# Stick-breaking items from the last query block down, and zeros and sums of h moved behind the head

## The chip, the cores and the metric

The kernel runs on one core of one Trainium2 chip. The metric is the device time of one launch, in microseconds (us). TensorE is called PE below, VectorE DVE, ScalarE ACT, GpSimd POOL, and SyncE, which issues nearly all DMAs, SP.

## The reference

The program is a trunk of two layers over 1024 tokens with 1024 features, in float32. Each layer is

```
h      = rmsnorm(x);  proj = h @ w_in            # q, k, v of two mixers, and two gates
o_a    = dilated sliding-window attention, 12 heads in 3 groups (dilation 1, 4, 16)
o_b    = stick-breaking attention, 4 heads:
         z = q k^T / 8,  for keys s < t only
         A[t,s] = sigmoid(z_ts) * prod_{s<j<t} (1 - sigmoid(z_tj))
         o = A v
x      = x + (sigmoid(g_a)*(o_a @ w_br_a) + sigmoid(g_b)*(o_b @ w_br_b)) @ w_o
x      = x + (gelu(causal_conv(h2 @ w_up_a)) * (h2 @ w_up_v)) @ w_down,   h2 = rmsnorm(x)
```

The product over j runs from the key to the query: for a query block, what a key's weight needs lies at later keys, and the scan runs from the last key down.

## The kernel before

Matmuls are made exact enough by splitting each operand into a high and a low part (`hi`, `lo`): ACT casts the high part, DVE or POOL subtracts it from the source for the low part, and PE runs three matmuls per pair (`product`). PE's instructions run in the order in which the Python program issues them (a manual schedule); DVE's, ACT's, POOL's and SP's order is set by a list scheduler with priorities, and each engine then works in order.

A layer's mixer has these parts.

- **Start and head.** In layer 0, `first` loads x, turns and normalises it into `h` (tiles `hh`, `hl`, one pair per half n of the tokens); a small tile `g_raw` holds the norm's gains. `head` makes values `v_ps` and the keys and queries (`kq_ps`, `q_ps`) of the first two stick heads by `kq_half`, one half of the tokens at a time, and writes them to DRAM (`sk`, `sq`, `sv`). In layer 1 the head is woven into the last products of the FFN before it (`d_ps`) and the norm (`nrm_t`).
- **Sums of h.** `block_sums` makes combinations of blocks of `h` for a seven-product (Strassen-like) scheme. Each of the first two series has four sums of three POOL instructions (`h_sum`), then a cast on ACT (`t_hi`) and a subtraction on DVE (`t_lo`). They are entries of `dense.side`, and one is taken with each `aside()`; before the change the head's loop calls `aside()` as well.
- **Zeros.** `zeros` (layer 0) fills a tile `none` with zeros and writes it to the unused parts of `sq` (8 DMAs) and `tk` (8 DMAs) in DRAM. It is called before the first part. `none` and `g_raw` share one buffer (tag "ot").
- **Dense units.** `Dense` hands out pieces of the big projections (`g_ps` plain, then `i_a`, `i_b`, `i_c` in seven products). One piece of six matmuls is a share. `advance(rate)` is called after each small step of attention and lets `rate` shares run; so dense matmuls fill PE while the attention's chain of ACT and DVE goes on.
- **Items.** `attend` runs 16 stick items, named by head u and pair qp of query blocks, then 4 windowed items (`near_item`, dilation 1), then 16 of the dilated groups. An item has scores and micro steps: `turn` (PE transposes 128 x 128 blocks into `sb_t`, then a split into parts) and `apply` (PE multiplies with the values into `sb_o`). The next item is scored while the present one is turned. A stick item's score gives `z`; ACT makes `beta` = sigmoid(z) and `stay` = sigmoid(-z); DVE scans `stay` from the last key down in chunks of up to 512 keys and multiplies `beta` by it.
- **Fetches.** `dense.fetch` issues the DMAs of an item's keys, queries and values (tiles `kv`, `slots`) once their data and room are there, and marks them as there (`FB`, `FN`) after `LEAD` = 6 further shares. A new head's rows are fetched only when all four items of the head before it are scored.

Before the change a head's items go qp = 0, 1, 2, 3, so from the shortest (256 keys) to the longest (1024), and an item's turns go from the first keys up. The first turn thus needs all scans of its two rows. `pair_v` transposes values (`v_t`), which shares a bank with the scores.

Of the kernel before, what the change touches and what calls it, by code (L numbers as in the profile page):

```python
# [16 lines left out]
P = 128  # L17
# [20 lines left out]
ET = mybir.EngineType  # L38
NO_SYNC = mybir.DependencyInfo(mybir.DependencyClass.NoSync, mybir.DependencyReason.DATA)
# [3 lines left out]
RATE = (1.0, 1.2, 1.35, 1.4)  # L43
RATE_N = 0.85
RATE_T = 0.8
PLAIN = 4
LEAD = 6
AHEAD_B = 3
# [10 lines left out]
def trunk_kernel(ctx, tc, x, norm1, w_in, b_gate, w_br, w_o, norm2, w_up, conv_w, conv_b, w_down, norm_f, out, depth=None, probe=None):  # L59
# [156 lines left out]
    class Dense:  # L216
# [4 lines left out]
        def __init__(self):  # L221
            self.main, self.plain, self.seven, self.done = [], [], [], set()
            self.side, self.later, self.hooks = [], {}, []
            self.now = self.nxt = None
            self.due, self.count = 0.0, 0
            self.started = False
            self.scored = self.applied = self.kq = self.v = 0
            self.rows, self.near, self.free = 0, 0, [0] * 4
            self.b = self.n = 0
# [25 lines left out]
        def fetch(self):  # L255
# [313 lines left out]
    def in_parts(c, scale, hi, lo, x):  # L569
        if c:  # L570
            act.mul(hi, x, scale)
            dve.scalar_tensor_tensor(lo, x, scale, f32(hi), ALU.mult, ALU.subtract)
        else:
            act.copy(hi, x)
            dve.tensor_tensor(lo, x, f32(hi), ALU.subtract)

    def kq_half(c, w, n):
# [3 lines left out]
        in_parts(c, SCALE, hi, lo, o)  # L581
# [52 lines left out]
    def fetch_row(j):  # L634

        u, qp = divmod(j, 4)
        if j == 0:
            R["kv"] = sb.tile([P, 2, T], F32R, tag="xa", bufs=4, name="kv")
        if "slots" not in R:
# [3 lines left out]
        nc.sync.dma_start(f32(R["slots"][:, j % 4]), sq[u][:, :, t])  # L643
        nc.sync.dma_start(f32(R["kv"][:, 1, t]).rearrange("p (b c) -> p b c", c=P), sv[u][:, 2 * qp : 2 * qp + 2, :])

    def fetch_whole(v):
        kv = R["kvn", v] = sb.tile([P, 2, T], F32R, tag="xa", bufs=4, name="kv")
        nc.sync.dma_start(f32(kv[:, 0, :]), sk[4 + v])
        for k in range(2):
            nc.sync.dma_start(f32(R["slots"][:, :, k, :]), sq[4 + v][:, k, :].rearrange("p (m c) -> p m c", c=256))  # L650
        nc.sync.dma_start(f32(kv[:, 1, :]).rearrange("p (b c) -> p b c", c=P), sv[4 + v])

    def stick_item(dense, u, qp):
        q, k, v = R["slots"][:, qp], R["kv"][:, 0, :], R["kv"][:, 1, :]
        pr, s = divmod(u, 2)
        rows, st, shared = {}, {}, {}

        def score(a):
            i = 2 * qp + a
            L = P * (i + 1)  # L660
# [4 lines left out]
            for c0 in range(0, L, 512):  # L665
                w = min(512, L - c0)
                z = bank("s", "z")
                scores(z[:, :w], *(q[:, x, a * P : a * P + P] for x in range(2)), k[:, c0 : c0 + w])
                with tc.high_priority(offset=AHEAD):
                    if c0 + w == L:  # L670
                        dve.tensor_tensor(z[:, w - P : w], z[:, w - P : w], mask_b, ALU.add)
                    act.activation(bt[:, c0 : c0 + w], z[:, :w], AF.Sigmoid)
                    act.activation(sv[:, c0 : c0 + w], z[:, :w], AF.Sigmoid, scale=-1.0)
# [8 lines left out]
        def scans(most=9):  # L682

            while SCANS and most:
                most -= 1
                bt, sv, c0, c1, L, soon = SCANS.pop(0)
                rev = sv[:, c0:c1][:, ::-1]
                with tc.high_priority(offset=AHEAD) if soon else nullcontext():
                    one = dve.tensor_tensor_scan(rev, rev, zero[:, 0:1].to_broadcast([P, c1 - c0]), 1.0 if c1 == L else sv[:, c1 : c1 + 1], ALU.mult, ALU.add)
                    if "dve" in LAST:  # L690
                        tc.add_manual_dep(one.ins, LAST["dve"], NO_SYNC, reason="in turn")
                    k0, k1 = max(0, c0 - 1), c1 - 1
                    dve.tensor_tensor(bt[:, k0:k1], bt[:, k0:k1], sv[:, k0 + 1 : k1 + 1], ALU.mult)

        def blocks(kb):

            return [(j, a) for j in range(2) for a in range(2) if kb + j <= 2 * qp + a]

        def turn(kb):
            if kb == 0:  # L700
                scans()
            tp = bank("t", "sb_t")
            todo = blocks(kb)
# [3 lines left out]
            scans(max(1, len(SCANS) - 2))  # L707

        def apply(kb):
            last = kb == 2 * qp  # L710
            if kb == 0:
                shared["o"] = bank("o", "sb_o")[:, :256]
            o = shared["o"]
            for j in range(2):
                c = P if last and j else 0
                for p in (0, 1):
# [4 lines left out]
                        start=(kb == 0 and j == 0 and p == 0),  # L721
                        stop=(last and j == 1 and p == 1),
                        skip_group_check=True,
                    )
            if qp == 3:
                dense.free[kb // 2] = u + 1
            if last:
# [5 lines left out]
        return sc, [(lambda kb=kb: turn(kb), lambda kb=kb: apply(kb)) for kb in range(0, 2 * qp + 2, 2)]  # L733
# [240 lines left out]
    def block_sums():  # L974
# [4 lines left out]
        def first(t, a, b, i):  # L979
# [6 lines left out]
            if "last" in keep:  # L986
                tc.add_manual_dep(one.ins, keep["last"], NO_SYNC, reason="one sum after the other")
            pool.tensor_tensor(r, r, f32(ah), ALU.add)
# [28 lines left out]
        series(set(), 3, lambda i: first(3, b22, b12, i), 4, 3)  # L1017
        series(set(), 1, lambda i: first(1, b12, b11, i), 4, 3)
        for i in range(4):
            todo.append((set(), lambda i=i: less(b22, i)))  # L1020
        series(set(), 2, lambda i: i or new_s(2), 0, 1)
        series({"plain"}, 4, lambda i: further(4, b21, i), 1, 1)
        return todo

    def zeros():
# [3 lines left out]
        for u in range(8):  # L1029
# [1033 lines left out]
```

## Time and profile before

| | |
|---|---|
| median of 3 runs | 2790.09 us (2789.9 to 2792.63) |
| profiled execution, own time | 2786.15 us |
| its span, first to last instruction | 2784.3 us |
| PE busy | 2658.9 us, 95% |
| DVE busy | 2082.1 us, 75% |
| ACT busy | 1343.6 us, 48% |
| POOL busy | 675.7 us, 24% |
| mean granted clock of PE | 0.987 |

The profile's views used below are: the page (busy times), the waits (whom an engine waited for: total us, times, longest), the timeline (start, duration, engine, line, output and inputs; in brackets the idle time before and what ended it), the view by stages (busy time per engine in a stretch, with the granted PE clock), and groups of instructions (busy us, mean ns, then idle time before them). Line numbers in them are those of the kernel before.

### The profile page before, as it was taken

How to read it: one execution, taken by the hardware profiler on the slowest of the kernel's cores; microseconds unless marked ns; L12 is line 12 of the kernel's file. 1: busy time of each engine (PE TensorE's matmuls, PEld its weight loads, DVE VectorE, ACT ScalarE, POOL GpSimd, SP SyncE). 2: the span in 40 equal slices, each digit the busy share in tenths (PEclk: the TensorE clock that was granted, in tenths of full speed). 3: DMA queues.
4: the chain of work that ended last, by engine and by line, in shares of the span. 5: the costliest groups of instructions: out<-in, count | busy, mean ns of one | idle time of the engine just before them, and what ended most of it. 6: DMA issues, size and time to landing. Idle time of an engine off the chain costs nothing. (4 is left out here: it accounts for less than half of the span.)

```text
span 2784.3 us, 36703 instructions
## 1 busy us (share of the span) xinstructions
PE 2658.9 (95%) x12780; PEld 2211.2 (79%) x12780; DVE 2082.1 (75%) x3151; ACT 1343.6 (48%) x2488; POOL 675.7 (24%) x481
## 2 busy tenths in 40 slices
PE   5899999999999999999979999999899999999999
PEld 5777777877888888888868777878788888888888
DVE  4677776568589889897656777656767888988965
ACT  4355555556455555532333555645554555554225
POOL 4300101103214334331060011011122334443210
PEclk9999999999999999999989999999999999999999
DMA  8545576566334444498534566656643344446863
GB/s 230 167 112 155 145 198 200 187 199 210 95 110 142 142 162 163 150 349 307 189 103 130 136 170 164 192 175 201 232 145 87 121 159 165 138 153 239 320 263 121
DMA packets 423140, 489.22 MB, mean 176 GB/s; under 512 B 26036, under 2 KB 339756, under 8 KB 421164
## 3 DMA queue, kind: packets, MB, share of 16 engines
q1 hardware_dynamic: 422940, 486.88, 54.5%
q8 instruction: 101, 1.65, 0.3%
q14 instruction: 83, 0.68, 0.1%
q10 hardware_dynamic: 16, 0.00, 0.0%
HBM read 311.62 MB, written 175.18 MB: 175 GB/s over the span
## 5 line engine op out<-in xcount | busy, mean ns | idle before, releaser
L144 DVE TENSOR_TENSOR w_lo<-up_a,w_hi 128x512 fp32r<-128x512 f32 x240 | 236.7, 992 | 20.1 <-ACT w_hi L139 20.1
L1058 POOL TENSOR_TENSOR u<-in_a 128x512 f32<-128x512 f32 x32 | 45.2, 1411 | 818.3 <-DMA in_a<-in_w_in_dram 275.8
L139 ACT CAST w_hi<-up_a 128x512 fp32r<-128x512 f32 x240 | 149.4, 622 | 183.8 <-PE u_a L969 45.9
L1699 DVE TENSOR_TENSOR x<-x,d_ps 128x512 f32<-128x512 f32 (+1 forms) x228 | 151.8, 671 | 77.5 <-PE d_ps L1693 76.0
L1430 POOL TENSOR_TENSOR cv<-cv 128x512 f32<-128x512 f32 x88 | 131.8, 1508 | 249.4 <-DVE cv L1425 139.5
L139 ACT CAST w_hi<-in_a 128x512 fp32r<-128x512 f32 x192 | 119.1, 620 | 150.2 <-PE i_a L969 50.4
L144 DVE TENSOR_TENSOR w_lo<-in_a,w_hi 128x512 fp32r<-128x512 f32 x192 | 139.2, 725 | 45.6 <-ACT w_hi L139 45.3
L144 DVE TENSOR_TENSOR g<-cv,g 128x512 fp32r<-128x512 f32 x154 | 151.7, 986 | 5.2 <-ACT g L139 2.8
L1691 PE MATMUL d_ps<-gd_in,w_hi 128*128 128x512 f32 (+1 forms) x340 | 130.4, 384 | 1.3 <-ACT w_hi L139 0.6
L1693 PE MATMUL d_ps<-gd_in,w_lo 128*128 128x512 f32 (+1 forms) x340 | 129.8, 382 | 0.0
L1692 PE MATMUL d_ps<-gd_in,w_hi 128*128 128x512 f32 (+1 forms) x340 | 129.7, 382 | 0.0
L968 PE MATMUL u_a<-hh,w_hi 128*128 128x512 f32 x320 | 124.7, 390 | 0.3
L970 PE MATMUL u_a<-t_hi,w_lo 128*128 128x512 f32 x320 | 124.5, 389 | 0.0
L970 PE MATMUL u_a<-hh,w_lo 128*128 128x512 f32 x320 | 124.5, 389 | 0.0
L969 PE MATMUL u_a<-t_lo,w_hi 128*128 128x512 f32 x320 | 124.5, 389 | 0.0
L969 PE MATMUL u_a<-hl,w_hi 128*128 128x512 f32 x320 | 124.5, 389 | 0.0
L968 PE MATMUL u_a<-t_hi,w_hi 128*128 128x512 f32 x320 | 124.5, 389 | 0.0
L144 DVE TENSOR_TENSOR w_lo<-w_raw,w_hi 128x512 fp32r<-128x512 f32 x96 | 71.0, 742 | 62.1 <-ACT w_hi L139 61.6
L139 ACT CAST g<-cv 128x512 fp32r<-128x512 f32 x154 | 94.9, 616 | 39.6 <-POOL cv L1430 29.2
L1691 PE MATMUL d_ps<-gd_in,wd 128*128 128x512 f32 (+1 forms) x292 | 113.9, 390 | 0.0
L1693 PE MATMUL d_ps<-gd_in,wd 128*128 128x512 f32 (+1 forms) x292 | 112.8, 386 | 0.0
L1692 PE MATMUL d_ps<-gd_in,wd 128*128 128x512 f32 (+1 forms) x292 | 112.8, 386 | 0.0
(393 smaller groups left out, 8581.1 us busy)
## 6 DMA issues: line engine op xcount, KB each, us to landing
gd<-g SPq DMA_DIRECT2D x154, 512.0 KB, 3.5
gd_in<-gd SPq DMA_DIRECT2D x154, 512.0 KB, 6.5
up_a<-in_w_up_dram SPq DMA_DIRECT2D x80, 512.0 KB, 5.3
in_a<-in_w_in_dram SPq DMA_DIRECT2D x64, 512.0 KB, 4.9
t_kq<-tk SPq DMA_DIRECT2D x32, 768.0 KB, 4.6
wd_raw<-in_w_down_dram SPq DMA_DIRECT2D x22, 1024.0 KB, 12.0
gin<-gs SPq DMA_DIRECT2D x32, 512.0 KB, 4.5
w_raw<-in_w_o_dram SPq DMA_DIRECT2D x64, 256.0 KB, 2.9
```

Source lines behind the costliest of these rows:

```text
L139: one = act.copy(hi, src)
L144: two = dve.tensor_tensor(lo, src, f32(hi), ALU.subtract)
L968: pe.matmul(o, w[0][:, c], rh, start=(first and i == 0), stop=False, skip_group_check=True)
L969: pe.matmul(o, w[0][:, c], rl, start=False, stop=False, skip_group_check=True)
L970: pe.matmul(o, w[1][:, c], rh, start=False, stop=(last and i == 3), skip_group_check=True)
L1058: pool.tensor_tensor(u2, a11, a21, ALU.subtract)
L1430: return lambda: pool.tensor_tensor(dst, a, b, ALU.subtract)
L1691: pe.matmul(o[:, sub], wh[:, c], gh[:, sub], start=(i == 0 and k in (0, 4, 5)), stop=False, skip_group_check=True)
L1692: pe.matmul(o[:, sub], wh[:, c], gl[:, sub], start=False, stop=False, skip_group_check=True)
L1693: pe.matmul(o[:, sub], wl[:, c], gh[:, sub], start=False, stop=(i == m - 1), skip_group_check=True)
L1699: dve.tensor_tensor(x, x, o[:, sub], ALU.add)
```

## The change

Seven edits go together.

1. A head's items go qp = 3, 2, 1, 0, and an item's turns from the last keys down; score chunks are cut from the last key, the last chunk of each row is scanned first, and a turn makes only the scans that its own keys need.
2. A head's keys and queries are fetched by quarters, each as soon as the item that used that quarter last is scored; values by quarters, when the last product with them is issued. An item still waits for all four quarters of its head.
3. The zero part of the queries is set once by a memset in `slots`, and only the other half is fetched; the 8 zero writes to `sq` go.
4. The remaining 8 zero writes (`tk`) become a side entry behind the first three series of sums, instead of the first thing issued.
5. The sums' first POOL instruction waits for the head's last `in_parts` (a real wait), and the head's loops no longer call `aside()`. Within the two series the steps are closer together (lag 3, gap 2 instead of 4, 3).
6. Windowed items are marked as fetched after 9 shares instead of 6; `pair_v` turns after 3 shares instead of 2, and its two copies get high priority.
7. Rates: 1.0, 1.15, 1.25, 1.3 for stick items (1.0, 1.2, 1.35, 1.4 before), 0.75 instead of 0.8 for the dilated groups.

```diff
+LEAD_N = 9
...
             def row(j):
-                u, qp = divmod(j, 4)
-                return j < 16 and {f"K{u}", f"V{u}"} <= self.done and (u == 0 or (self.rows >= 4 * u and self.free[qp] >= u))
+                return j < 16 and f"K{j // 4}" in self.done and self.rows >= j - 3
+
+            def row_v(j):
+                return j < self.b and self.free[3 - j % 4] >= j // 4
...
+            while row_v(self.bv):
+                fetch_values(self.bv)
+                self.bv += 1
             while whole(self.n):
                 fetch_whole(self.n)
-                self.at(LEAD, lambda v=self.n: self.done.add(f"FN{v}"))
+                self.at(LEAD_N, lambda v=self.n: self.done.add(f"FN{v}"))
...
-        in_parts(c, SCALE, hi, lo, o)
+        LAST["head"] = in_parts(c, SCALE, hi, lo, o).ins.name
...
     def fetch_row(j):
-        u, qp = divmod(j, 4)
+        u, qp = j // 4, 3 - j % 4
...
+            pool.memset(f32(R["slots"][64:128, :, 1, :]), 0.0)
         t = slice(256 * qp, 256 * qp + 256)
         nc.sync.dma_start(f32(R["kv"][:, 0, t]), sk[u][:, t])
-        nc.sync.dma_start(f32(R["slots"][:, j % 4]), sq[u][:, :, t])
+        nc.sync.dma_start(f32(R["slots"][:, qp, 0, :]), sq[u][:, 0, t])
+        nc.sync.dma_start(f32(R["slots"][0:64, qp, 1, :]), sq[u][0:64, 1, t])
+
+    def fetch_values(j):
+        u, qp = j // 4, 3 - j % 4
+        t = slice(256 * qp, 256 * qp + 256)
         nc.sync.dma_start(f32(R["kv"][:, 1, t]).rearrange("p (b c) -> p b c", c=P), sv[u][:, 2 * qp : 2 * qp + 2, :])
...
     def stick_item(dense, u, qp):
...
-            for c0 in range(0, L, 512):
-                w = min(512, L - c0)
+            for c1 in range(L, 0, -512):
+                c0 = max(0, c1 - 512)
+                w = c1 - c0
...
-            for c1 in range(L, 0, -512):
-                SCANS.append((bt, sv, max(0, c1 - 512), c1, L, False))
-            if L <= 512:
-                scans()
+                (SCANS if c1 == L else left).append((shared, bt, sv, c0, c1, L))
             if a:
-                dense.rows = 4 * u + qp + 1
+                SCANS.extend(left)
+                dense.rows += 1
...
         def turn(kb):
-            if kb == 0:
-                scans()
+            while any(x[0] is shared and x[4] > kb * P for x in SCANS):
+                scans(1)
...
-            scans(max(1, len(SCANS) - 2))
+            scans(2)
...
         def apply(kb):
-            last = kb == 2 * qp
-            if kb == 0:
+            first = kb == 2 * qp
+            if first:
                 shared["o"] = bank("o", "sb_o")[:, :256]
+                dense.free[qp] = u + 1
...
-        return sc, [(lambda kb=kb: turn(kb), lambda kb=kb: apply(kb)) for kb in range(0, 2 * qp + 2, 2)]
+        return sc, [(lambda kb=kb: turn(kb), lambda kb=kb: apply(kb)) for kb in range(2 * qp, -2, -2)]
...
             if "last" in keep:
                 tc.add_manual_dep(one.ins, keep["last"], NO_SYNC, reason="one sum after the other")
+            else:
+                tc.add_manual_dep(one.ins, LAST["head"], SYNC, reason="after the first projections")
...
-        series(set(), 3, lambda i: first(3, b22, b12, i), 4, 3)
-        series(set(), 1, lambda i: first(1, b12, b11, i), 4, 3)
+        series(set(), 3, lambda i: first(3, b22, b12, i), 3, 2)
+        series(set(), 1, lambda i: first(1, b12, b11, i), 3, 2)
...
         series(set(), 2, lambda i: i or new_s(2), 0, 1)
+        todo += more
...
     def zeros():
...
-        for u in range(8):
-            nc.sync.dma_start(sq[u][64:128, 1, :], none[0:64].rearrange("p a b -> p (a b)"))
...
-            act.copy(vv[:, :, :, 0:64], tw)
-            dve.tensor_tensor(vv[:, :, :, 64:128], tw, f32(vv[:, :, :, 0:64]), ALU.subtract)
+            with tc.high_priority(offset=AHEAD):
+                act.copy(vv[:, :, :, 0:64], tw)
+                dve.tensor_tensor(vv[:, :, :, 64:128], tw, f32(vv[:, :, :, 0:64]), ALU.subtract)
...
-            dense.at(2, lambda: turn(c, n, f))
+            dense.at(3, lambda: turn(c, n, f))
...
-        dense.side = block_sums()
+        dense.side = block_sums([(set(), zeros)] * (l == 0))
...
             for _ in units:
-                dense.aside()
+                pass
         else:
-            zeros()
...
             for _ in first_units:
-                dense.aside()
+                pass
...
-            items.append((f"B{j // 4}{j % 4}", [f"FB{j}"], [], RATE[j % 4], lambda j=j: stick_item(dense, j // 4, j % 4)))
+            items.append((f"B{j}", [f"FB{j // 4 * 4 + 3}"], [], RATE[3 - j % 4], lambda j=j: stick_item(dense, j // 4, 3 - j % 4)))
```

More of the change, by code (lines that the diff above doesn't have):

```diff
@@ L571, in in_parts @@
             act.mul(hi, x, scale)
[L572 to L575, printed above, removed]
+            return dve.scalar_tensor_tensor(lo, x, scale, f32(hi), ALU.mult, ALU.subtract)
+        act.copy(hi, x)
+        return dve.tensor_tensor(lo, x, f32(hi), ALU.subtract)
     def kq_half(c, w, n):
@@ L679, in score, with scans @@
+                (SCANS if c1 == L else left).append((shared, bt, sv, c0, c1, L))
             if a:
-                dense.rows = 4 * u + qp + 1
-        def scans(most=9):
+                SCANS.extend(left)
+                dense.rows += 1
+        def scans(most):
             while SCANS and most:
                 most -= 1
-                bt, sv, c0, c1, L, soon = SCANS.pop(0)
+                _, bt, sv, c0, c1, L = SCANS.pop(0)
                 rev = sv[:, c0:c1][:, ::-1]
[L688 to L693, printed above, removed]
@@ L695, in blocks @@
-        def blocks(kb):
-            return [(j, a) for j in range(2) for a in range(2) if kb + j <= 2 * qp + a]
+                one = dve.tensor_tensor_scan(rev, rev, zero[:, 0:1].to_broadcast([P, c1 - c0]), 1.0 if c1 == L else sv[:, c1 : c1 + 1], ALU.mult, ALU.add)
+                if "dve" in LAST:
+                    tc.add_manual_dep(one.ins, LAST["dve"], NO_SYNC, reason="in turn")
+                k0, k1 = max(0, c0 - 1), c1 - 1
+                dve.tensor_tensor(bt[:, k0:k1], bt[:, k0:k1], sv[:, k0 + 1 : k1 + 1], ALU.mult)
@@ L720, in apply @@
                         shared[kb][p][:, 256 * j : 256 * j + 256 - c],
-                        start=(kb == 0 and j == 0 and p == 0),
-                        stop=(last and j == 1 and p == 1),
+                        start=(first and j == 0 and p == 0),
+                        stop=(kb == 0 and j == 1 and p == 1),
                         skip_group_check=True,
                     )
-            if qp == 3:
-                dense.free[kb // 2] = u + 1
-            if last:
+            if kb == 0:
                 out_ = small("ob")[0:64, 0:256]
```

30 lines of the change are left out of this document (15 added, 15 removed).

## The prediction

> **What bounds the kernel now.** I read the page's busy times first, then the waits of the tensor engine (PE), then the timeline where each long wait ends.
>
> ```profile
> span 2784.3 us, 36703 instructions
> PE 2658.9 (95%) x12780; PEld 2211.2 (79%) x12780; DVE 2082.1 (75%) x3151; ACT 1343.6 (48%) x2488; POOL 675.7 (24%) x481
> ```
>
> PE is busy 95% of the span, and the change issues the same matmuls (the built program's order lists as many rows on PE before and after, and the same dense matmuls per layer). So what can be won is PE's idle time, 2784.3 - 2658.9 = 125 us, and stretches in which PE runs at a lower clock. Who ends the idle time:
>
> ```profile
> PE warm L1967 <- DMA g_raw<-in_norm_dram: 25.7, 1, 25.7
> PE sb_t L705 <- DVE beta L693: 17.7, 14, 3.2
> PE nrm_t L506 <- DVE nrm L459: 11.9, 2, 11.8
> PE z L613 <- DMA kv<-sk: 9.5, 2, 5.2
> PE z L613 <- DVE vv L1153: 7.3, 6, 2.0
> PE kq_ps L176 <- DVE vb L550: 5.8, 1, 5.8
> PE kq_ps L177 <- POOL hl L523: 5.5, 2, 4.7
> PE v_t L1149 <- DVE u L1088: 5.2, 4, 2.4
> PE v_ps L176 <- DVE kq_l L572: 5.0, 1, 5.0
> ```
>
> These nine rows make 93.6 us, and the edits touch all of them. After a long wait PE also runs slowly. In the view by stages (columns: length, then busy time of PE, its weight loads, DVE, ACT, POOL, then granted clock, DMA share, GB/s):
>
> ```profile
> 74.00:100.00 26.00, 15.18 (x69) 13.58 (x68) 20.63 (x21) 5.49 (x10) 18.56 (x12) 0.74 0.41 111
> 450.00:466.00 16.00, 10.82 (x45) 8.66 (x44) 6.72 (x14) 4.29 (x11) 0.13 (x1) 0.79 0.61 175
> 1410.00:1462.00 52.00, 34.71 (x155) 29.42 (x154) 23.25 (x29) 15.79 (x27) 30.69 (x22) 0.77 0.40 114
> 1818.00:1834.00 16.00, 11.68 (x48) 9.42 (x47) 7.52 (x14) 4.63 (x11) 1.33 (x2) 0.79 0.70 206
> ```
>
> Length times the missing clock gives what the slow clock costs behind these waits: 26 x 0.26 = 6.8 us (head of layer 0), 52 x 0.23 = 12.0 us (entry of layer 1), and 16 x 0.21 = 3.4 us each in front of a windowed item.
>
> **Part 1, zeros out of the start.** The queues at the start:
>
> ```profile
> 0.74 0.39 SPq L1880 DMA_DIRECT2D xr<-in_x_dram  x1
> 1.95 8.87 SPq L1030 DMA_DIRECT2D sq<-none  x8
> 10.86 9.99 SPq L1034 DMA_DIRECT2D tk<-none  x8
> 20.90 2.40 SPq L1883 DMA_DIRECT2D w_raw<-in_w_in_dram  x2
> 24.58 0.58 ACTq L1869 DMA_DIRECT2D g_raw<-in_norm_dram  x1
> 29.69 0.27 PE L1967 MATMUL warm<-ident,g_raw 8*128 8x8 f32 x1 [25.74 <-DMA g_raw<-in_norm_dram]
> 34.80 0.39 PE L176 MATMUL v_ps<-w_hi,hh 128*128 128x256 f32 x1
> ```
>
> Sixteen writes of zeros hold SP from 1.95 to 20.85 us, ahead of the first weights. `g_raw` is on ACT's queue, but it lies in the same single buffer (tag "ot") as the tile of zeros, so its load starts at 24.58 and lands at 29.69, 5.1 us later. After the change the eight `sq` writes are gone and the eight `tk` writes stand behind the sums of h. `g_raw` can then start at about 0.7 and land by 5.8; the two weights start at about 1.2 instead of 20.90, 19.7 us earlier. From `g_raw` to the first projection lie 34.80 - 29.69 = 5.1 us, so the projection would start near 10.9 by `g_raw`, near 15.1 if the weights' place alone counted (34.80 - 19.7). The weights' casts were through well before 34.80, so I take `g_raw`: **-24 us** (19.7 to 26).
>
> **Part 2, sums of h behind the head.** In layer 0:
>
> ```profile
> 67.88 0.39 PE L178 MATMUL q_ps<-hh,kq_w 128*128 128x512 f32 x1
> 73.37 0.62 ACT L139 CAST t_hi<-h_sum 128x512 fp32r<-128x512 f32 x1 [3.38 <-POOL h_sum L989]
> 76.05 0.59 ACT L571 ACTIVATE kq_h<-q_ps 128x512 fp32r<-128x512 f32 x1
> 78.28 0.68 DVE L572 SCALAR_TENSOR_TENSOR kq_l<-q_ps,kq_h 128x512 fp32r<-128x512 f32 x1
> ```
>
> `q_ps` is complete at 68.3, but ACT reads it only at 76.05: ACT works in order and stood at `t_hi` casts that wait for POOL's sums. DVE's `kq_l` ends at 78.96, and PE's 5.0 us wait ends with it. The 5.8 us wait for `vb` has the same origin. With the sums held back by the dependency on the head's last `in_parts`, both go, and the slow clock behind them: 5.0 + 5.8 + 6.8 = 17.6; I leave 1 us: **-16.6** (10 to 17.6). Layer 1, where the sums mix with the norm:
>
> ```profile
> 1403.61 0.39 PE L1693 MATMUL d_ps<-gd_in,w_lo 128*128 128x512 f32 x1
> 1414.08 0.62 ACT L139 CAST t_hi<-h_sum 128x512 fp32r<-128x512 f32 x1 [4.74 <-POOL h_sum L989]
> 1414.52 0.67 DVE L1699 TENSOR_TENSOR x<-x,d_ps 128x512 f32<-128x512 f32 x1
> 1419.54 0.68 DVE L1699 TENSOR_TENSOR x<-x,d_ps 128x512 f32<-128x512 f32 x1
> ```
>
> PE's last `d_ps` ends at 1404.0, yet DVE adds it at 1419.54, queued behind work on sums that waits for ACT and POOL. That is the 11.8 us wait at `nrm_t`; the two waits for POOL's `hl` (5.5) come from `hl` queued between sums. 11.8 + 5.5 + 12.0 = 29.3; the chain of `hl` may become late next, so I leave 1.3: **-28** (20 to 29.3).
>
> Of the moved work every instruction still runs: per layer 24 sums on POOL, eight casts on ACT, eight subtractions on DVE, now beside the first stick items. What that costs there:
>
> ```profile
> L988 POOL TENSOR_TENSOR h_sum<-h_sum,hh 128x512 f32<-128x512 f32 x8 | 12.9, 1612 | 0.6
> L144 DVE TENSOR_TENSOR t_lo<-h_sum,t_hi 128x512 fp32r<-128x512 f32 x7 | 7.9, 1147 | 3.8 <-ACT t_hi L139 3.6
> 125.61 0.68 DVE L144 TENSOR_TENSOR t_lo<-h_sum,t_hi 128x512 fp32r<-128x512 f32 x1
> ```
>
> Beside POOL's sums DVE's `t_lo` takes 1.15 us, alone 0.68: 0.47 more. The built order puts about 30 DVE instructions of that kind (subtractions, scans, products of two SBUF tiles) beside the sums in layer 0: 30 x 0.47 = 14 us of DVE. Layer 1 starts its sums 11 us earlier relative to the items and overlaps less. Some of this lies in DVE's idle time, so I take **+8** for both layers (0 to 28). The Trainium skill ("GPSIMD Engine Reference", Specifications) says that GpSimd's SBUF interfaces are shared with VectorE, contended by instructions with two SBUF inputs; that speaks against this move. The trace agrees: the longer `t_lo` above.
>
> One wait is new. In layer 0 ACT's third `t_hi` stands ahead of the cast of the second gate's weights. Three sums of three POOL instructions (1.3 to 1.6 us each) end 12 to 14.5 us after the head, near 121; cast and subtraction follow, while PE asks near 119. That is about 3 us, and the slow clock behind it 0 to 3.4 (the 450:466 row); I take **+4.7** (0 to 8). The Trainium skill ("TensorE: Matmul & The Clock Gate", Part 1) gives an idle window of about 3.4 us before the clock halves; by it the second piece would be 0 and the total 1.7 us lower.
>
> **Part 3, items from the last block down.** Times of one instruction over all shapes (min/median/max ns):
>
> ```profile
> L689 DVE TENSOR_TENSOR_SCAN stay<-stay,zero x96: 414/1211/2118, 121.2 to 1737.6; 128x512 f32<-128x512 f32 x48, 128x128 f32<-128x128 f32 x16, 128x256 f32<-128x256 f32 x16, 128x384 f32<-128x384 f32 x16
> L693 DVE TENSOR_TENSOR beta<-beta,stay x96: 273/674/1687, 121.7 to 1739.9; 128x512 f32<-128x512 f32 x32, 128x127 f32<-128x127 f32 x16, 128x255 f32<-128x255 f32 x16, 128x383 f32<-128x383 f32 x16
> L672 ACT ACTIVATE beta<-z x96: 256/546/620, 120.7 to 1730.3; 128x512 f32<-128x512 f32 x48, 128x128 f32<-128x128 f32 x16, 128x256 f32<-128x256 f32 x16, 128x384 f32<-128x384 f32 x16
> ```
>
> A turn needs two sigmoids (1.1), a scan (1.2) and a product (0.7): 3.0 us behind its scores, 3.3 with the mask. Counting PE's instructions between score and first turn in the built orders, two of four items per head had only 3 to 4.4 us before; now it is one per head with 3.3 to 3.8 us, and the other three have nearly 7 us or more. The remaining turns wait for fewer chunks. Of 17.7 us I leave 8, about 1 us per head: **-10** (-17.7 to +5).
>
> The longer leads: `v_t` asked 5.2 us too early and moves one share (six matmuls, 1.4 us) later; `vv`'s high priority frees the bank that scores wait for (7.3). I take **-8** of 12.5 (4 to 12.5). Windowed items wait 9.5 + 2 x 3.4 for `kv`; three more shares are 4.2 us against waits of up to 5.2: **-14** (5 to 16.3).
>
> Against that, the first item now needs the last quarter of the queries:
>
> ```profile
> 107.72 0.68 DVE L572 SCALAR_TENSOR_TENSOR kq_l<-q_ps,kq_h 128x512 fp32r<-128x512 f32 x1
> 113.59 1.23 SPq L643 DMA_DIRECT2D slots<-sq  x2
> L613 PE MATMUL z<-kv,slots x160: 220/328/522, 118.3 to 1840.4; 128*128 128x256 f32 x72, 128*128 128x512 f32 x48, 128*128 128x128 f32 x24, 128*128 128x384 f32 x16
> slots<-sq SPq DMA_DIRECT2D x14, 256.0 KB, 3.6
> ```
>
> `kq_l` ends at 108.4, the fetch follows at 113.59 and lands 3.6 us later; its second DMA, issued 0.6 later, lands near 118, and PE asks at 118.3. The margin is nearly zero: **+2** for both layers (0 to 12). At later heads the last quarter is fetched six shares (8 us) ahead, more than that landing. Splitting the query fetch adds 16 DMAs per layer to SP, about 0.6 us each by the row above (1.23 for two), and the eight `tk` writes now hold SP for 10 us in the stick stage of layer 0; both lie in SP's idle time as long as that lead covers them, and (d) below is the case where it doesn't. The retuned rates shift dense work; the built order has the same rows after the last dense matmul, but for four, so I cost them at nothing.
>
> **Sum.** -24 - 16.6 - 28 - 10 - 8 - 14 = -100.6; +8 + 4.7 + 2 = +14.7; net -86. The profiled execution took 2786.15 us, the median of the runs is 2790.09, 3.9 above it. 2786.15 - 86 + 3.9 = **2704 us**.
>
> **Rivals.** (a) Forecast, gains as summed: 2704, chance 0.68. (b) DVE becomes the bound beside the moved sums: all 28 us reach PE, and slow clock behind them in the head's ratio (6.8 on 10.8 us of wait, 0.6) adds 17; 45 instead of 8 is +37: 2741 at its end, 2725 halfway. For it: DVE is 75% busy; against: the stick stage's turns have slack now. Chance 0.20. (c) The start does not shrink, since the first loads are late anyway: 2728. Against it: `xr` is issued at 0.74 already and nothing else stands ahead. Chance 0.05. (d) Slower: every head now begins with its longest item, and SP is the one queue for its quarters. If other DMAs stand ahead at each head, as the eight `tk` writes with 9.99 us would, the 8 us lead is gone: 10 us plus 3.4 of slow clock at eight heads is 107 us, 2811. It decides from 86 / 8 = 11 us per head. Against it: those writes occur once. Chance 0.04. (e) All waits vanish without new ones: 2690. Chance 0.03.
>
> The range 2684 to 2740 reaches from full gains in the head, entry and start to (b)'s end. Within 0.2% (5.6 us, about what a measurement of this kernel can tell from no change) almost nothing lies: faster 0.95, same 0.01, slower 0.04.
>
> **What would show it.** Right: `g_raw` lands before 7 us and the first projection starts near 11; no PE wait over 2 us at `nrm_t`, `kq_ps`, `v_ps`; clock 1.0 at layer 1's entry; `sb_t` under 10 us in total. Wrong: DVE's two-input instructions at 1.3 us or more beside POOL's sums with PE waiting for `beta` or for gate weights (b), or PE at `z` waiting for `slots` at head after head (d).

## The result, and the profile after

| | before | changed |
|---|---|---|
| median of the runs (us) | 2789.99 (2789.6 to 2792.63, 4 runs) | 2719.29 (2717.83 to 2722.56, 4 runs) |
| ratio, 95% interval | | 0.9746, 0.9729 to 0.9763 |
| profiled execution / its span (us) | 2786.15 / 2784.3 | 2720.71 / 2718.9 |
| mean granted clock | 0.987 | 0.992 |

The change is faster by 70.7 us. 86 were forecast; 2719.29 lies inside the forecast range of 2684 to 2740. Between the profiled spans lie 65.4 us, and the stages and waits below are parts of these spans. The head of the page:

```profile
span 2718.9 us, 36768 instructions
PE 2648.2 (97%) x12780; PEld 2204.5 (81%) x12780; DVE 2079.8 (76%) x3151; ACT 1341.5 (49%) x2488; POOL 680.1 (25%) x483
```

The waits of the tensor engine (what waits, what releases it; us in total, times, longest):

```profile
PE z L619 <- ACT stay L685: 15.8, 12, 7.0
PE o L888 <- ACT p1h L141: 9.2, 8, 1.9
PE sb_t L709 <- DVE beta L701: 8.6, 10, 1.7
...
PE z L619 <- DVE vv L1158: 1.0, 1, 1.0
...
PE nrm_t L513 <- DVE nrm L466: 0.2, 1, 0.2
```

PE has the same 12780 matmuls; its idle time went from 125 to 70.7 us. Every wait that the prediction named is gone or halved: `g_raw` 25.7 and `kv` 9.5 have no row, `nrm_t` 11.9 is 0.2, `sb_t` 17.7 is 8.6, `vv` 7.3 is 1.0. But two rows that were at the bottom of the list before now lead it: `z` behind ScalarE's `stay` and `o` behind ScalarE's `p1h` (the high part of the weights of a dilated item, cast by ScalarE). In the trace of before they read:

```profile
PE z L613 <- ACT stay L673: 2.2, 4, 1.3
PE o L885 <- ACT p1h L139: 1.7, 6, 0.4
```

That is 13.6 and 7.5 us of new waiting. The start, in the timeline of the changed kernel:

```profile
0.74 0.59 ACTq L1873 DMA_DIRECT2D g_raw<-in_norm_dram  x1
...
3.15 0.27 PE L1971 MATMUL warm<-ident,g_raw 8*128 8x8 f32 x1
...
4.38 1.06 ACT L1914 ACTIVATE xsq<-xr 128x1024 f32<-128x1024 f32 x1 [1.51 <-DMA xr<-in_x_dram]
...
8.35 0.39 PE L178 MATMUL v_ps<-w_hi,hh 128*128 128x256 f32 x1
```

`g_raw` is issued at 0.74 as forecast, but has landed by 3.15 instead of 5.8: at most 2.4 us after its issue, where it took 5.1 in the kernel before. From there to the first projection it is 5.2 us, about as before, but by another chain: the gains are spread (`gb`) by 5.66, while the norm waits for the first tile of x, which ScalarE reads at 4.38, and goes on at 6.16. So loading x bounds the start now, and no longer `g_raw`. The stages (length, busy time of PE, its weight loads, DVE, ACT, POOL, then the granted clock, DMA share and GB/s): head of layer 0, the 58 us behind it, and head of layer 1.

```profile
8.40:76.00 67.60, 67.38 (x428) 59.84 (x428) 36.09 (x87) 34.86 (x69) 21.89 (x20) 1.00 0.85 263
76.00:134.30 58.30, 47.02 (x218) 38.04 (x216) 50.27 (x61) 26.75 (x52) 33.83 (x21) 0.91 0.42 118
1366.30:1424.80 58.50, 58.26 (x355) 52.02 (x354) 24.87 (x38) 17.16 (x30) 27.20 (x20) 1.00 0.61 171
```

Both heads now run PE without a gap at full clock. The stage between them and the dense matmuls by seven products (from the first score `z` to the first `i_a`; below "plain stage") is where the moved work landed. Before it was 48.8 us long, with POOL busy for 7.02 us of it instead of 33.83. In it the timeline shows three engines at once:

```profile
78.86 0.62 ACT L141 CAST t_hi<-h_sum 128x512 fp32r<-128x512 f32 x1 [3.20 <-POOL h_sum L994]
79.39 1.13 ACT L141 CAST w_hi<-w_raw 128x512 fp32r<-128x512 f32 x2
80.43 0.58 ACT L1198 COPY gt<-g_ps 128x512 f32<-128x512 f32 x1
81.02 1.28 ACT L684 ACT_TABLE_LOAD   x1
82.32 0.49 ACT L684 ACTIVATE beta<-z 128x384 f32<-128x384 f32 x1
...
80.53 3.41 DVE L146 TENSOR_TENSOR w_lo<-w_raw,w_hi 128x512 fp32r<-128x512 f32 x2
...
85.30 2.20 DVE L697 TENSOR_TENSOR_SCAN stay<-stay,zero 128x512 f32<-128x512 f32 x1 [1.15 <-ACT stay L685]
...
87.60 1.51 DVE L701 TENSOR_TENSOR beta<-beta,stay 128x512 f32<-128x512 f32 x1
...
85.32 0.80 PE L619 MATMUL z<-kv,slots 128*128 128x512 f32 x1 [7.00 <-ACT stay L685]
...
101.15 0.50 PE L619 MATMUL z<-kv,slots 128*128 128x512 f32 x1 [3.08 <-ACT stay L685]
```

The first row is the third `t_hi` that the prediction named: ScalarE stands 3.20 us for POOL's sum, and the gate weights, the table load and the first sigmoids stand behind it. PE's first scores end at 76.9 and fill both score banks, the six dense matmuls behind them end at 78.3, and PE gets a bank back at 85.32. And VectorE's instructions with two operands in SBUF run long beside the sums: a scan of 2.20 and a product of 1.51, where the same shapes (128x512) take 1.22 and 0.68 in the mean in this stage when the sums run in the head (second experiment).

### The profile page after: what moved, and what is told of

Its sections match the earlier page's. It is cut to its first block, busy times and chain, and to the rows that moved or that the text cites. A ratio compares the mean times of both kernels' runs of the same rounds, so it can differ in the third digit from the quotient of the medians.

```text
span 2718.9 us, 36768 instructions
## 1 busy us (share of the span) xinstructions
PE 2648.2 (97%) x12780; PEld 2204.5 (81%) x12780; DVE 2079.8 (76%) x3151; ACT 1341.5 (49%) x2488; POOL 680.1 (25%) x483
```

## The experiments

The interval of one ratio is about 0.002 to either side, 5 us; each ratio is to the kernel before on the same chip. The code lines are cuts from each run's edit, with comments added and `...` for what is left out; `span +18.3` means against the changed kernel's 2718.9. Stage lengths (us) are cut at the same marks in each profiled trace: first `v_ps`, first `z` and first `i_a` of each layer, and the first `br_ps` behind all attention items. The row of items thus ends with the dilated groups ("far stage" below).

| stage | before | changed | zeros first | sums in head | old stick edits | a third of the sums | early sums, zeros behind |
|---|---|---|---|---|---|---|---|
| start | 34.8 | 8.4 | 33.9 | 9.0 | 8.8 | 8.5 | 8.6 |
| head, layer 0 | 83.5 | 67.6 | 67.2 | 84.0 | 67.5 | 67.4 | 67.5 |
| plain stage, layer 0 | 48.8 | 58.3 | 58.7 | 46.2 | 61.5 | 46.2 | 46.4 |
| items, layer 0 | 460.4 | 454.8 | 455.6 | 454.7 | 457.3 | 455.4 | 459.5 |
| to layer 1 | 776.4 | 777.2 | 776.9 | 776.7 | 775.7 | 775.2 | 775.4 |
| head, layer 1 | 82.6 | 58.5 | 58.4 | 80.9 | 58.4 | 58.2 | 58.3 |
| plain stage, layer 1 | 49.1 | 47.5 | 47.5 | 44.7 | 50.1 | 44.7 | 44.8 |
| items, layer 1 | 459.9 | 456.9 | 457.3 | 451.3 | 464.8 | 454.3 | 457.9 |
| rest | 788.8 | 789.8 | 788.8 | 789.5 | 789.4 | 789.2 | 790.7 |
| span | 2784.3 | 2718.9 | 2744.3 | 2737.2 | 2733.6 | 2699.1 | 2709.0 |

**Zeros first.**

```
 first_units = relay(head(l))          # with, ahead of it:
+zeros()                               # and in zeros(), eight writes sq <- none
-dense.side = block_sums([(set(), zeros)] * (l == 0))
+dense.side = block_sums([])
```

> The changed kernel, with only the zeros back at the start (eight writes of sq and eight of tk ahead of the first loads). Theory (the start is bound by the tile that g_raw shares with the zeros): the first projection starts near 34.8 us instead of 8.4, everything behind it is shifted by the same, and the time is 24 to 26 us above the changed kernel, near 2744; the zeros' share of SP in the stick stage of layer 0 is worth less than 2 us there. Rival (the eight tk writes, now in the stick stage of layer 0, are what makes that stage 4 us longer): the start costs 26, that stage gives 4 or more back, and the time is near 2740 or lower.

Measured: 2747.05 us, ratio 0.9861 (0.9847 to 0.9875); span 25.4 above the changed kernel's, 25.5 of it in the start. The items of layer 0 did not get shorter. The theory holds: the start is worth what its own wait was, and the eight `tk` writes in the stick stage cost nothing that shows.

**Sums in the head again.**

```
-else: tc.add_manual_dep(one.ins, LAST["head"], SYNC, ...)
-series(set(), 3, ..., 3, 2)   +series(set(), 3, ..., 4, 3)     # and t = 1
-for _ in units: pass          +for _ in units: dense.aside()   # both layers
```

> The changed kernel, with only the sums of h back in the head (no dependency on the last projection, lag and gap 4 and 3, asides in the head). Theory (the gains in the heads are the sums' alone, and their price is paid in the plain stage of layer 0): head 0 is near 83 us again (+16), the entry of layer 1 near 82 (+24), the plain stage of layer 0 falls from 58 to about 49 (-9 to -10), and the sum is about +30, near 2750. Rival (the longer plain stage of layer 0 comes from the new order of items, not from the sums): the plain stage stays near 58 us and the time is near 2759.

Measured: 2739.0 us, ratio 0.9834 (0.982 to 0.9848), span +18.3. The heads lose 16.4 and 22.4 us. The plain stages give back 12.1 and 2.8, and the items of layer 1 another 5.6: the sums cost about 20 us where they now stand, so that +18.3 came instead of +30. Against the kernel before, this run also shows what the stick edits bring while the sums stay in the head: the span is 47.1 us shorter, 25.8 of it in the start, so 21.3 elsewhere. The rival (the order of items makes the plain stage longer) is refuted: with the same order it is 46.2 us. The waits that return are those of before:

```profile
PE nrm_t L513 <- DVE nrm L466: 12.3, 2, 12.1
...
PE z L619 <- ACT stay L685: 7.1, 13, 1.6
PE kq_ps L178 <- DVE vb L557: 5.9, 1, 5.9
PE kq_ps L179 <- POOL hl L530: 5.5, 2, 4.7
PE v_ps L178 <- DVE kq_l L579: 5.3, 1, 5.3
```

and `z` behind `stay` falls from 15.8 to 7.1. `o` behind `p1h` does not: it is 9.3 here and 9.2 in the changed kernel, so that wait is not the sums'.

**A third of the sums.**

```
-pool.tensor_tensor(r, r, f32(ah), ALU.add)
-keep["last"] = pool.tensor_tensor(r, r, f32(bh), ALU.subtract).ins.name
+keep["last"] = one.ins.name
```

> The changed kernel with one GpSimd instruction per sum of h instead of three; it leaves two of every three out, so it does not compute the reference. Theory (the price of the moved sums is how long GpSimd holds them: t_hi stands on ScalarE until the sum is there, the cast of the gate weights and the sigmoids stand behind it, VectorE is slowed beside it): the tensor engine's gap of 11.3 us in the plain stage of layer 0 falls to 3 to 4, its half clock there from 5.1 to 0, and the time by 10 to 14, to about 2707. Rival (the stage is bound by the two score banks and the chain of sigmoid, scan, product and not by the sums): the gap stays at 9 us or more and the time within 4 us of the changed kernel.

Measured: 2702.67 us, ratio 0.9703 (0.9689 to 0.9717), span -19.8, more than the expected 10 to 14. The plain stage of layer 0, in the view by stages:

```profile
75.90:122.10 46.20, 43.94 (x217) 35.60 (x216) 37.73 (x58) 25.69 (x50) 8.07 (x6) 1.00 0.48 137
```

With sixteen of 24 POOL instructions gone per layer, this stage is 12.1 us shorter and its clock 1.00; VectorE is busy 37.73 us in it instead of 50.27. Here the same casts are still on ScalarE. What the moved sums cost is the time in which POOL holds them.

**Casts later.**

```
-series(set(), 3, lambda i: first(3, b22, b12, i), 3, 2)
+series(set(), 3, lambda i: first(3, b22, b12, i), 6, 2)
```

> The changed kernel, with the casts of the first series of sums six steps behind their sums instead of three: GpSimd works as long and as early as in the changed kernel, but ScalarE no longer reaches a t_hi whose sum isn't there. Theory (the wait of 7.0 us at z is ScalarE standing at t_hi, ahead of the gate weights and the sigmoids): the plain stage of layer 0 falls from 58 to 48 to 51 us and its half clock to 0 or 1.7; the time is 6 to 11 below the changed kernel. Rival (VectorE's slower scans and subtractions beside the sums are the cost): the stage stays above 54 us with waits at sb_t for beta, and the time within 3 us of the changed kernel.

Measured: 2721.19 us, ratio 0.9762 (0.9744 to 0.978). This is the experiment that was to tell the two halves of that cost apart, ScalarE standing at `t_hi` and VectorE slowed by POOL, and it gave both theories half. Without the third `t_hi` in the way the wait of 7.00 us is 2.76, and the plain stage 53.3 us instead of 58.3 (48 to 51 expected, above 54 by the rival); but 3.1 us of wait behind the slow scans stay, and the items behind get 4.7 us longer, 2.3 of it a new wait of `i_c` for ScalarE's `gt`. In total nothing is won.

**Sums one product earlier.**

```
+one = in_parts(c, SCALE, hi, lo, o)
+if c == 0: LAST["head"] = one.ins.name     # last key half, not last query half
```

> The changed kernel, with the sums of h released one product earlier, after the last half of the keys instead of the last query product (some 5.5 us). Theory (the third sum is late for ScalarE by the wait of 7.0 us at z and the 3.1 us behind it): the first of these waits falls to 1.5 to 3, the half clock of 5.1 in the plain stage of layer 0 falls to 1.7 or nothing, the head stays at 67.6, and the time is 5 to 10 below the changed kernel. Rival (VectorE's slower instructions beside the sums are the cost, whenever they run): the wait only moves, and the time is within 3 us of the changed kernel, or above it if the head's own subtraction is held up.

Measured: 2714.81 us, ratio 0.9738 (0.9719 to 0.9757), span 2715.5. The wait of 7.0 became 3.7 and the plain stages 55.4 and 44.9. That is the direction of the theory but not its size: 1.5 to 3 was expected for the wait, at least 5 for the time. The 3.4 us of the spans cannot be told from nothing by the ratio.

**Old stick edits** (items from the first block up, old fetches, leads, priority and rates; zeros and sums as in the changed kernel).

> The kernel before, with the zeros and the sums moved as in the changed kernel, but items, fetches, leads, priority and rates as before: what the stick edits bring together is the difference between this and the changed kernel. Theory (start and heads bring 66 us, the price in the plain stage of layer 0 is about 10, and the stick edits bring far less than the 30 us that I summed for them): near 2733, 10 to 18 us above the changed kernel. Rival (the stick edits bring their 30 us and the moved sums cost 20 more in the stick stages than assumed): near 2749.

Measured: 2735.63 us, ratio 0.9818 (0.9804 to 0.9833), span +14.7 against the changed kernel. With the sums moved, the stick edits bring 14.7 us together, half of the 30 that I summed and what this run's theory expected.

**Their three parts, one at a time.**

```
-LEAD_N = 9    -dense.at(3, ...)    -with tc.high_priority(...)    # leads back
-RATE = (1.0, 1.15, 1.25, 1.3); RATE_T = 0.75                      # rates back
+RATE = (1.0, 1.2, 1.35, 1.4); RATE_T = 0.8
-u, qp = j // 4, 3 - j % 4       -for c1 in range(L, 0, -512)      # order back
+u, qp = divmod(j, 4)            +for c0 in range(0, L, 512)
```

> The changed kernel with the three leads as before (windowed fetch 6 shares ahead instead of 9, v_t after 2 shares instead of 3, no priority for the copies into vv). Forecast by my terms: 8 for v_t and vv and 14 for kv come back, +22. Theory after seeing the changed kernel's trace (the waits at v_t and vv are worth 3 and 6, and the one for kv is partly given back in the far stage): +8 to +14, with kv waits of up to 5 us and one more half clock in each layer. Rival (the leads do nothing, the new order of items removed these waits): within 3 us of the changed kernel and no wait at z for kv.

> The changed kernel with the rates of dense work as before (1.0, 1.2, 1.35, 1.4 and 0.8). In the changed kernel the windowed far stage has 9.1 and 7.8 us of gaps and 4.5 and 5.5 us of half clock, where the kernel before had 5.7 and 6.1 with 3.4 and 3.2. Theory (the lower rates leave dense work for later but spread it thinner, so that the last windowed items wait for ScalarE): with the old rates the far stages' gaps change by 2 us or more, and the time by 2 to 6 in either direction. Rival (I costed the rates at nothing): within 2 us of the changed kernel and the far stages as they are.

> The changed kernel with items, item parts and fetches in the order of before (from the first query block up, queries in the same fetch as keys and values), with the new leads and rates. The stick edits together brought 14.7 (2733.6 against 2718.9), the rates going back cost 8.5, the leads going back nothing. Theory (the parts add up: the order alone is worth about 6, most of it as fewer waits at sb_t for beta, which were 20.1 with the old order and 8.6 with the new): a span near 2725, sb_t at 17 to 20 again. Rival (the rates only pay with the new order, since a thinner spread of dense work leaves the old order's short items less cover): a span of 2732 or more.

> The changed kernel itself once more, on the same chip as the two kernels beside it. Both theories: a ratio of 0.973 to 0.976 to the kernel before, a profiled span of 2716 to 2721.

Measured: leads back 2717.38 us, ratio 0.9751 (0.9731 to 0.977); rates back 2726.07, ratio 0.9779 (0.976 to 0.9798); order back 2720.39, ratio 0.9771 (0.975 to 0.9791), beside the changed kernel again, on the same chip, with 2718.36, ratio 0.9767 (0.9745 to 0.9788). So the leads alone bring nothing that shows and the order alone some 2 us that could be nothing; the rates alone bring about 7 by the medians (2726.07 against 2718.36 and 2719.29), at the edge of what the intervals tell apart. My expectations of +8 to +14 for the leads and of 6 for the order were too high, that of 2 to 6 for the rates a little low. Taken off one at a time the three come to less than the 14.7 us that they bring together; the rest was not split further. The waits of PE say why so little; leads back, then order back:

```profile
PE o L888 <- ACT p1h L141: 3.8, 2, 2.3
PE z L620 <- DMA slots<-sq: 3.0, 4, 1.2
PE z L619 <- DMA slots<-sq: 3.0, 2, 2.0
```

```profile
PE sb_t L709 <- DVE beta L697: 26.1, 18, 4.4
PE z L614 <- ACT stay L677: 10.0, 6, 5.3
...
PE o L889 <- ACT p1h L141: 0.4, 2, 0.2
```

With the old leads PE waits 6.0 us for `slots`, and 5.4 us less for `p1h` than in the changed kernel: what the earlier fetch wins is waited for elsewhere. With the old order it waits 26.1 instead of 8.6 us at `sb_t`, but 5.8 less at `z` and 8.8 less at `o`. By stages, the old order is 5.0 and 5.7 us longer in the two plain stages (63.3 and 53.2) and 3.4 and 9.3 shorter in the items (451.4 and 447.6): the new order wins early and gives it back late. With the old rates it is PE's waits at `j_ps` that rise:

```profile
PE j_ps L942 <- DVE on L946: 5.5, 2, 2.8
PE j_ps L942 <- POOL fx L928: 4.5, 2, 2.4
```

In the changed kernel those are 2.3 and 2.2. The dense work that covers such waits is used up earlier with the old rates: its last matmul starts 39.9 and 39.1 us before the first `br_ps` of the two layers, against 25.6 and 25.3 in the changed kernel.

**Early sums.** This run and the next look for a version that keeps both gains: sums on POOL in the head, but their casts on ScalarE behind it.

```
+one = in_parts(c, SCALE, hi, lo, o); LAST["end"] = one.ins.name
+if (c, n) == ((0, 1) if HEADL[0] else (1, 0)): LAST["head"] = one.ins.name
 # in split(), for the casts of sums:
+tc.add_manual_dep(one.ins, LAST[behind], SYNC, ...)       # behind = "end"
```

> The changed kernel with the sums on GpSimd released inside the head, after the first query half in layer 0 (some 22 us earlier) and after the last key half in layer 1 (some 5 us earlier), while ScalarE's casts of them are held back to the head's last product. Theory (the price of the moved sums is their time on GpSimd beside the first items, and the price in the head was only ScalarE's casts standing in it): the head of layer 0 stays at 67 to 69 us, the plain stage of layer 0 falls from 58.3 to 47 to 51, and the span is 8 to 13 below the changed kernel, 2706 to 2711. Rival (the sums cost their time wherever they run, since VectorE's subtractions in the head are slowed too): the head grows by 4 us or more and the span is within 4 of the changed kernel.

Measured: 2714.24 us, ratio 0.9749 (0.9729 to 0.9768), span 2710.5; plain stage 53.8 instead of 47 to 51. The span lies in the expected 2706 to 2711, but not for the expected reason. POOL's timeline shows that only two of the sums' instructions ran early:

```profile
44.71 1.29 POOL L995 TENSOR_TENSOR h_sum<-hl 128x512 f32<-128x512 f32 x1 [14.14 <-DVE kq_l L581]
46.08 1.30 POOL L1000 TENSOR_TENSOR h_sum<-h_sum,hh 128x512 f32<-128x512 f32 x1
66.29 0.95 POOL L1041 MEMSET none<- 64x1024 f32 x1 [18.91 <-DMA w_raw<-in_w_in_dram]
67.20 1.28 POOL L1001 TENSOR_TENSOR h_sum<-h_sum,hh 128x512 f32<-128x512 f32 x1
```

The memset of the zeros' tile was third in POOL's order and waited there 18.9 us. Its tile lies in the single buffer under the tag "ot", and the tile there before it is `raw_c`; in the changed kernel the same memset starts at 65.08, released by PE's `pt_c`, which reads `raw_c`. (The row above names a DMA; releasers are inferred.) It is the old start's fault once more, on another queue, and the next run tests it.

**Early sums, zeros behind four of them.**

```
+clear = pool.memset(none[0:64], 0.0)
+tc.add_manual_dep(clear.ins, LAST["fourth"], NO_SYNC, ...)   # last instruction of sum 4
```

> The early sums of h once more, with the memset of the zeros' tile placed behind the fourth sum on GpSimd. In the run before it stood third on GpSimd's queue and waited there until 66.3 us (18.9 us idle), so that only two of the sums' 24 instructions ran in the head of layer 0. Here four sums, twelve instructions of 1.29 us, should end near 60 us, ahead of ScalarE's first t_hi, and the last sum near 90 instead of 104. Theory (what is left of the plain stage's loss is ScalarE standing at t_hi and VectorE slowed by sums that run too late): no t_hi waits for h_sum, the waits of 3.7 and 3.1 us at z fall below 1.5 each, the plain stage goes from 53.8 to 46 to 49 us, the head stays at 67 to 69, and the span is 2702 to 2707. Rival (VectorE and GpSimd slow each other in the head as much as behind it): the head grows by what the plain stage loses and the span stays at 2709 to 2712.

Measured: 2708.56 us (2705.55 to 2710.84, 5 runs), ratio 0.9714 (0.9699 to 0.973): faster than the changed kernel, by some 10 us of the medians, and the fastest version with all of the sums (the two intervals just touch). POOL and ScalarE in the timeline, then the plain stage in the view by stages:

```profile
43.93 1.30 POOL L995 TENSOR_TENSOR h_sum<-hl 128x512 f32<-128x512 f32 x1 [14.44 <-DVE kq_l L581]
...
59.33 1.75 POOL L1001 TENSOR_TENSOR h_sum<-h_sum,hh 128x512 f32<-128x512 f32 x1
...
66.29 1.66 ACT L141 CAST t_hi<-h_sum 128x512 fp32r<-128x512 f32 x3 [1.18 <-DVE kq_l L581]
```

```profile
76.10:122.50 46.40, 43.98 (x217) 35.59 (x216) 40.59 (x56) 25.60 (x50) 17.98 (x11) 1.00 0.48 136
```

Four sums are done at 61.1; three `t_hi` run in a row, waiting for no sum. The plain stage is as short as with a third of the sums, and the head stays at 67.5, of which VectorE is busy for 39.5 (36.1 in the changed kernel): it has room there. So the rival falls by the head, though the profiled span of 2709.0 lies at the edge of its 2709 to 2712; the profiled run is the slowest of the five, and the median of their spans, 2706.8, lies in the expected 2702 to 2707. Of the 11.9 us won in the plain stage, 4.7 went in the items of layer 0. There the clock has three steps of 3.41 us at half speed that the changed kernel doesn't have (from 137.2, 229.3 and 563.8 us), worth at most 1.7 us each; why PE pauses ahead of them stays open.

## Why the prediction was right, and where not

| term | forecast | measured | by |
|---|---|---|---|
| zeros out of the start | -24 | -26.4 | stage (-25.4 by the first experiment) |
| head of layer 0 | -16.6 | -15.9 | stage (-16.4 with the sums moved back) |
| entry of layer 1 | -28 | -24.1 | stage (-22.4 with the sums moved back) |
| price of the moved sums | +12.7 | +15.5 | old stick edits against before, less the three rows above it |
| stick edits | -30 | -14.7 | changed against old stick edits |
| sum | -86 | -65.6 | spans: -65.4 |

The measured terms add up to the difference of the spans, so the 20 us that are missing can be placed: 15.3 of them are Part 3. The price row is -50.7 (2733.6 - 2784.3) plus the 66.2 that start and heads bring in that kernel. But the last two rows hang on the order in which the edits are taken off. With the sums in the head the stick edits bring 21.3, and under the new stick edits the moved sums cost 20.5 (12.1 + 2.8 + 5.6, second experiment). By that order Part 3 misses by 8.7 and the price by 7.8. Some 6 us thus belong to neither alone: the moved sums eat a part of what the stick edits win. Both orders have the stick edits well short of 30 and the price above 12.7.

**Start and heads** were right in mechanism and nearly in size. The start won 2.4 more, since `g_raw` landed faster than the row of before said; that loading x would be next there, some 0.5 us behind, was not foreseen and cost little by luck. The entry of layer 1 was mis-sized by 3.9 of slow clock. I priced it as window length times missing clock, 52 x 0.23 = 12.0, and added the waits. But PE was busy for only 34.71 of those 52 us, and a slow clock costs nothing while PE waits: 34.71 x 0.23 = 8.0. With that the sum is 17.3 + 8.0 = 25.3, and the stage lost 24.1. The head of layer 0 does not decide between the two ways: 15.18 x 0.26 = 3.9 in place of 6.8 makes 14.7 in place of 17.6, and the stage lost 15.9.

**The price of the sums** was too low (15.5 or 20.5 against 12.7), and both mechanisms were there: the third `t_hi` (3 us forecast, 3.20 measured) and VectorE's longer instructions. What I had wrong is who waits. I expected PE to wait for gate weights; it waits for a score bank, 7.00 us, since ScalarE's sigmoids stand behind the same cast. Rival (b) shows in its own sign, VectorE at 1.5 to 2.2 us beside the sums, but at a third to under a half of its price of 45, and PE waits for `beta` only 1.2 us in that stage. The Trainium skill ("GPSIMD Engine Reference", Specifications) names this contention without a price. The trace agrees: VectorE is busy 12.5 us less in this stage (three instructions fewer, 58 for 61) when two thirds of the sums' work is left out. How the price divides between the two mechanisms was not settled.

**Part 3 is the step that failed.** The waits did go as it says: `sb_t` -9.1, `vv` -6.3, `kv` -9.5. I then counted them as time and did not ask what would be late next. ScalarE was late next: `z` behind `stay` and `o` behind `p1h` took 13.6 and 7.5 (10.1 of the 13.6 belong to the plain stage, and so to the sums). The slow clock in front of the windowed items, 2 x 3.4 us by my price, did go: from 105.7 to 580 us the clock is 1.00. But it came back in the far stage. In layer 0, before and after:

```profile
610.00:630.00 20.00, 16.02 (x90) 13.02 (x90) 16.86 (x38) 11.98 (x29) 3.13 (x4) 0.83 0.78 281
572.00:602.00 30.00, 22.83 (x102) 18.23 (x102) 24.79 (x48) 19.29 (x37) 5.39 (x5) 0.77 0.68 244
```

By PE's busy time that is 16.02 x 0.17 = 2.7 us before and 22.83 x 0.23 = 5.3 after; layer 1 goes the same way, 2.7 to 5.6. With the 7.5 us of `o`, which is waited for in the same stage, some 13 us came back of the 14 that I forecast for the windowed items. That fits the run with the old leads, which lost nothing.

And the one part that I costed at nothing, the rates, is the one that alone shows an effect, about 7 us. The same rows after the last dense matmul did not mean that the rows before it cover waits equally well.

Rivals (c), (d) and (e) are out: the start shrank, no row of waits for `slots` appears, and new waits came. The time lies between the forecast (a) and halfway to (b). That halfway point is 2704 + 18.5 = 2722.5, not 2725. And the range's lower end does not come out of the reason given for it: full gains in head, entry and start take only 4.3 off 2704, to 2699.7. Neither slip bears on the outcome.

## What to carry to other kernels

Work taken off a critical head is not free where it lands: look which in-order queue it enters there, and what stands behind it. Here POOL could do four of layer 0's sums inside the head without lengthening it; only their casts on ScalarE had to wait. A wait that a longer lead or another order removes is a gain only up to the next-late engine, so read the list of waits down to its small rows before adding up the large ones. And price a slow clock on PE's busy time, not on the length of the window: idle time in it is counted already as a wait.

## What the hardware showed

The half clock comes in steps of 3.41 us on a fixed grid. With the windows of the changed kernel cut on that grid:

```profile
78.39:81.80 3.41, 0.00 (x0) 0.00 (x0) 2.28 (x2) 2.92 (x5) 3.26 (x3) 1.00 0.08 20
81.80:85.22 3.42, 0.00 (x0) 0.00 (x0) 2.35 (x3) 2.03 (x5) 3.33 (x3) 0.50 0.47 137
85.22:88.63 3.41, 3.31 (x8) 2.63 (x9) 3.33 (x3) 1.34 (x4) 3.33 (x3) 0.50 0.93 265
88.63:92.04 3.41, 3.19 (x15) 2.10 (x13) 3.31 (x3) 1.44 (x4) 3.33 (x2) 1.00 0.78 208
...
98.87:102.28 3.41, 1.13 (x6) 1.00 (x7) 3.41 (x5) 1.41 (x4) 1.72 (x2) 1.00 0.22 50
102.28:105.70 3.42, 3.42 (x12) 2.83 (x11) 3.42 (x4) 1.61 (x4) 3.26 (x3) 0.50 0.32 96
```

A step in which PE was busy 0.00 or 1.13 us is followed by one at 0.50; one with 3.31 by one at 1.00. In the kernel with the later casts a wait of 3.11 us, as long as the 3.08 us here, fell across two steps, and the clock stayed:

```profile
92.04:95.45 3.41, 1.81 (x10) 1.19 (x8) 3.41 (x2) 0.59 (x1) 3.08 (x2) 1.00 0.86 228
95.45:98.87 3.42, 1.91 (x9) 1.64 (x10) 3.30 (x7) 2.56 (x6) 0.00 (x0) 1.00 0.03 10
98.87:102.28 3.41, 3.41 (x18) 2.87 (x18) 3.27 (x5) 2.49 (x6) 2.58 (x2) 1.00 0.60 185
```

In the far stage of the changed kernel this step, idle for 1.80 us, is followed by one at 0.50:

```profile
576.78:580.20 3.42, 1.62 (x10) 1.18 (x10) 1.77 (x5) 2.31 (x7) 0.00 (x0) 1.00 0.66 261
```

So in these traces a step that is idle for about half its length can be enough, and the same wait costs 0 or 1.7 us by where it falls. The border is not sharp: above, 1.60 idle us kept the clock, and in the last experiment a step with 1.44 (from 560.4 us) lost it; the ends of matmuls are modelled. The Trainium skill ("TensorE: Matmul & The Clock Gate", Part 1) has a free-running window of that length, which the trace shows too, but asks for a whole idle window; here 2.28 idle us of 3.41 did it, and the measurement decides.
